# Up-projections of two gated FFNs by seven block products for eight, down-projections woven between them, and buffers that the stages share

## The chip, the cores and the metric

One core of one Trainium2 chip. The metric is the device time of one execution in microseconds; the time before is the median of three runs. Engines: PE is TensorE (PEld its weight loads), DVE is VectorE, ACT is ScalarE, POOL is GpSimd, SP is SyncE, which issues the transfers of weights.

## The reference

A decoder trunk of two layers on 512 tokens of 1024 features, all in float32. Layer 0 mixes by a causal Conformer convolution, layer 1 by sparse attention; each is followed by a gated FFN with 2816 features. All are residual blocks behind an RMS norm. What the change touches:

```python
def conv_ffn(h, w_up, w_dw, b_dw, w_down):
    a, v = jnp.split(h @ w_up, 2, axis=-1)
    return (jax.nn.silu(causal_dwconv(a, w_dw, b_dw)) * v) @ w_down

def reference(x, ...):
    for i in range(DEPTH):
        h = rmsnorm(x, mix_norm_g[i])
        if i % N_MIXERS == 0:
            x = x + conformer_conv(h, ...)
        else:
            x = x + nsa_attention(h, ...)
        x = x + conv_ffn(rmsnorm(x, ffn_norm_g[i]), ...)
    return x
```

`causal_dwconv` in the FFN adds three taps along the tokens, per feature.

## The kernel before

The program runs four stages one after the other: the convolution module (to about 190 us), the first FFN (to about 608), attention (to about 956) and the second FFN. Features lie on the 128 partitions and tokens on the free axis, so the residual stream is eight tiles `x` of 128x512.

Products keep float32 accuracy by an exact split: every weight and activation is the sum of a high part (a cast on ACT, L202 and L208) and a low part (a subtraction on DVE, L203 and L209; in attention some on POOL), and each product is three matmuls: high x high, high x low, low x high (`mm3`, L212 to L215). A load of weights, `load_split`, is a DMA on SP's queue into one of 3 raw buffers, the cast into one of 4 `wh` and the subtraction into one of 4 `wl`. These buffers belong to one pool `wp`, which all stages share.

`ffn` goes through the 22 feature tiles of 128 in chunks of 8, 8 and 6. For a tile f it loads the weights of its two halves (`a` and `v`, L519 on), and multiplies each by the 8 tiles of the normed input: 2 x 8 x 3 = 48 matmuls of 512 columns into PSUM banks pf and pa. The norm's denominators come later: after the first half of tile 0 `finish` and `spread` form 1/rms per token, which multiplies the result (`nrm.b`). Then the activation chain: `a` and `vv` are products of PSUM and `nrm.b` on DVE (L529, L531), the first tap and the bias on ACT (L530), two taps on DVE (L532, L534), Silu on ACT (L536), the product with `vv` on DVE (L537), and the split. When a chunk's tiles are done, each of 8 output tiles m adds up 24 (last chunk 18) matmuls in PSUM bank pb, 8 m's per chunk, and DVE adds it to x[m] (L546). An FFN has 528 such matmuls in all. In the last chunk x[m] goes on to the next stage's norm (`Norm.add`: scaled high part on ACT L231, low part on DVE L232, square on ACT L237, sum of squares on POOL L248), or to the output.

Attention ends with its out-projection: the last 39 matmuls wait for the last head's values (L956 adds their results to x on DVE).

The instructions of all stages go into one program. Within it each engine works through its own list in order, and the lists are set when the program is built: a tile framework takes the operations, and orders ready ones for each engine, so that work of the next loop step or of the next stage can stand before work of this one, as far as buffers of the pools are free. A buffer of a pool is given to the next tile that asks when its last reader is done. The rows of such lists, with the tiles' names and running numbers, are shown below.

Of the kernel before, what the change touches and what calls it, by code (L numbers as in the profile page):

```python
# [18 lines left out]
P = 128  # L19
# [7 lines left out]
CHUNKS = [range(0, 8), range(8, 16), range(16, 22)]  # L27
# [10 lines left out]
# columns of the packed per-feature vectors  # L38
# [14 lines left out]
# columns of the packed token-major tables  # L53
# [11 lines left out]
# order of the work beside the heads: first step and advance per step (a head takes six steps)  # L65
# [59 lines left out]
def _program(tc, A, stop=None, dbg=None):  # L125
    nc = tc.nc
    es = ExitStack()
    with es:
        const = es.enter_context(tc.tile_pool(name="const", bufs=1))
        wp = es.enter_context(tc.tile_pool(name="wp", bufs=1))  # L130
        sp = es.enter_context(tc.tile_pool(name="sp", bufs=51))
        sm = es.enter_context(tc.tile_pool(name="sm", bufs=1))
        psp = es.enter_context(tc.tile_pool(name="psp", bufs=1, space=bass.MemoryType.PSUM))

# [23 lines left out]
        for k in range(KT):  # L158
            nc.sync.dma_start(x[k], A["xT"][k * P:(k + 1) * P, :])
            if k in FIRST_W:  # L160
                raw = wp.tile([P, WPW], F32, tag="raw", name=nm("raw"), bufs=3)
                nc.sync.dma_start(raw[:, :1024], A["pw1"][len(first)])
                first.append(raw)
# [9 lines left out]
        # keeps TensorE's clock up while it has nothing else to do  # L173
        idle = const.tile([P, S], F32R, name="idle")
        nc.vector.memset(idle.bitcast(F32), 0.0)

        def warm(n, tag, after=None):
            """products without a use, that follow the tile `after`"""
# [15 lines left out]
        def load_split(src, n=1024, eng=None):  # L194
            if first:
                raw = first.pop(0)
            else:
                raw = wp.tile([P, WPW], F32, tag="raw", name=nm("raw"), bufs=3)
                nc.sync.dma_start(raw[:, :n], src)
            h = wp.tile([P, WPW], F32R, tag="wh", name=nm("wh"), bufs=4)  # L200
            l = wp.tile([P, WPW], F32R, tag="wl", name=nm("wl"), bufs=4)
# [16 lines left out]
        class Norm:  # L218
# [16 lines left out]
            def square(s, k):  # L235
# [3 lines left out]
                if s.two:  # L239
                    # even tiles on GpSimd, odd ones on VectorE  # L240
# [11 lines left out]
            def sums(s, q, start, stop):  # L252
                """adds q over the features, one column per 128 tokens"""
# [6 lines left out]
            def finish(s):  # L260
                """mean square and its root, per token"""
# [10 lines left out]
        def spread(tok, tag):  # L272
            """the [128, 4] values of the tokens as a row in every partition, in PSUM"""
# [11 lines left out]
        def conv_module(nrm, nxt):  # L285
# [18 lines left out]
            class Unit:  # L304
                """one tile of features: gated unit, then 31 taps shared between the engines: TensorE adds its taps
# [896 lines left out]
```

## Time and profile before

| | us |
|---|---|
| three runs, median (range) | 1336.77 (1333.28 to 1338.4) |
| profiled execution: its time and span | 1333.7 |
| PE busy | 1287.4 (97%) |
| DVE busy | 857.9 (64%) |
| ACT busy | 626.8 (47%) |
| POOL busy | 356.6 (27%) |

The profile gives one execution: for each engine its busy time and number of instructions, the chain of work that ended last followed back to the start, groups of instructions by program line with the mean duration of one, and for any stretch of time the busy time of each engine in it, PE's granted clock (1.00 is full speed) and the share of the DMA engines. In a group or timeline row the brackets, or what stands behind the last bar, tell how long the engine was idle before it and what ended that. A row with x2 joins two instructions.

### The profile page before, as it was taken

The numbers are of one execution on the slowest core, as the hardware profiler recorded it, in microseconds if no ns is written. First come the engines' busy times: TensorE is split into PE (matmuls) and PEld (weight loads), VectorE is DVE, ScalarE is ACT, GpSimd is POOL, SyncE is SP. The second block draws the span as 40 slices with busy tenths as digits, with TensorE's granted clock in tenths as the row PEclk, the third lists the DMA queues.
The fourth block names the chain that finished last, engine by engine and source line by source line (L and its number), as shares of the span: only waits on it lengthen the run. The fifth ranks groups of instructions, "written<-read, shape, count | busy, mean of one in ns | idle before, by whom it ended". The sixth has DMA issues, their size and how long they took to land.

```text
span 1333.7 us, 16982 instructions
## 1 busy us (share of the span) xinstructions
PE 1287.4 (97%) x6314; PEld 1073.6 (80%) x6314; DVE 857.9 (64%) x1429; ACT 626.8 (47%) x1151; POOL 356.6 (27%) x430
## 2 busy tenths in 40 slices
PE   8999789999999999999899999999999999999998
PEld 6887678888888888878789898887788888888886
DVE  6999964665455535554878889788756535553552
ACT  7677543443233323342567788776643313331330
POOL 3669931000000000032467667743400000000000
PEclk9999879999999999999899999999999999999999
DMA  6122101433333333235241111110033322233321
GB/s 235 45 63 64 48 6 58 127 95 95 95 95 95 95 95 96 78 112 149 79 156 35 33 33 50 33 46 33 16 95 95 96 95 94 95 98 95 95 80 76
DMA packets 32321, 109.13 MB, mean 82 GB/s; under 512 B 3696, under 2 KB 4336, under 8 KB 32240
## 3 DMA queue, kind: packets, MB, share of 16 engines
q1 hardware_dynamic: 32240, 108.05, 25.9%
q8 instruction: 50, 0.82, 0.3%
q14 instruction: 31, 0.25, 0.1%
HBM read 103.85 MB, written 2.10 MB: 79 GB/s over the span
## 4 chain that ended last, share of the span: by engine, by line
PE 80%; DVE 9%; POOL 5%; ACT 4%; issue 2%; DMA 0%; SPq 0%; ACTq 0%; POOLq 0%; DVEq 0%
PE pf L213 11%; PE pf L215 11%; PE pf L214 11%; PE pb L213 7%; PE pb L215 7%; PE pb L214 7%; PE pa L215 6%; PE pa L213 6%; PE pa L214 6%; PE po L930 2%; POOL s L344 2%; PE pb L914 1%; DVE s L209 1%; DVE pa L895 1%; DVE s L626 1%
## 5 line engine op out<-in xcount | busy, mean ns | idle before, releaser
L202 ACT CAST wh<-raw 128x1024 fp32r<-128x1024 f32 (+2 forms) x196 | 202.1, 1033 | 398.6 <-PE pb L214 156.2
L203 DVE TENSOR_TENSOR wl<-raw,wh 128x1024 fp32r<-128x1024 f32 (+2 forms) x179 | 223.1, 1248 | 55.2 <-ACT wh L202 54.7
L213 PE MATMUL pf<-s,wh 128*128 128x512 f32 x600 | 236.3, 397 | 6.0 <-DVE s L325 2.3
L215 PE MATMUL pf<-s,wl 128*128 128x512 f32 x600 | 237.9, 396 | 0.5 <-DVE wl L203 0.5
L214 PE MATMUL pf<-s,wh 128*128 128x512 f32 x600 | 238.0, 397 | 0.0
L213 PE MATMUL pa<-s,wh 128*128 128x512 f32 x368 | 145.0, 395 | 0.0
L215 PE MATMUL pa<-s,wl 128*128 128x512 f32 x368 | 145.0, 394 | 0.0
L213 PE MATMUL pb<-s,wh 128*128 128x512 f32 x368 | 144.2, 394 | 0.6 <-DVE x L546 0.6
L215 PE MATMUL pb<-s,wl 128*128 128x512 f32 x368 | 144.7, 393 | 0.0
L214 PE MATMUL pa<-s,wh 128*128 128x512 f32 x368 | 144.6, 393 | 0.0
L214 PE MATMUL pb<-s,wh 128*128 128x512 f32 x368 | 144.5, 393 | 0.0
L213 PEld LDWEIGHTS pf<-s,wh 128*128 128x128 f32 x600 | 113.6, 190 | 31.7 <-DVE s L325 2.6
L248 POOL TENSOR_TENSOR s<-s,s 128x512 f32<-128x512 f32 x18 | 28.2, 1564 | 402.2 <-DVE s L232 333.6
L215 PEld LDWEIGHTS pf<-s,wl 128*128 128x128 f32 x600 | 114.0, 190 | 26.4 <-DVE wl L203 1.0
L214 PEld LDWEIGHTS pf<-s,wh 128*128 128x128 f32 x600 | 114.1, 190 | 25.3 <-issue 0.2
L546 DVE TENSOR_TENSOR x<-pb,x 128x512 f32<-128x512 f32 x48 | 33.0, 692 | 141.0 <-PE pb L215 141.0
L906 POOL TENSOR_SCALAR s<-s,cf,gates 128x128 f32<-128x128 f32 (+3 forms) x128 | 80.1, 633 | 79.1 <-DVE cf L903 68.2
L529 DVE TENSOR_TENSOR s<-pf,s 128x512 f32<-128x512 f32 x44 | 30.4, 691 | 93.3 <-PE pf L215 86.6
L213 PE MATMUL pf<-wh,s 128*128 128x256 f32 (+1 forms) x288 | 83.9, 292 | 4.6 <-DVE v L731 2.9
L214 PE MATMUL pf<-wl,s 128*128 128x256 f32 (+1 forms) x288 | 82.9, 288 | 0.0
L213 PEld LDWEIGHTS pb<-s,wh 128*128 128x128 f32 x368 | 69.2, 188 | 17.0 <-DVE x L546 1.5
L215 PE MATMUL pf<-wh,s 128*128 128x256 f32 (+1 forms) x288 | 82.8, 288 | 0.0
(214 smaller groups left out, 2498.3 us busy)
## 6 DMA issues: line engine op xcount, KB each, us to landing
raw<-in_up_dram SPq DMA_DIRECT2D x88, 512.0 KB, 3.5
raw<-in_dn_dram SPq DMA_DIRECT2D x32, 512.0 KB, 3.5
raw<-in_pw_dram SPq DMA_DIRECT2D x24, 512.0 KB, 3.5
raw<-in_dn_dram SPq DMA_DIRECT2D x16, 384.0 KB, 3.0
raw<-in_win_k_dram SPq DMA_DIRECT2D x8, 536.0 KB, 3.6
raw<-in_win_q_dram SPq DMA_DIRECT2D x8, 512.0 KB, 3.6
raw<-in_cw_dram SPq DMA_DIRECT2D x8, 512.0 KB, 3.7
raw<-in_wout_dram SPq DMA_DIRECT2D x8, 512.0 KB, 3.7
```

Of the source, the lines that this page charges most:

```text
L202: nc.scalar.copy(h[:, :n], raw[:, :n])
L203: (eng or nc.vector).tensor_sub(l[:, :n], raw[:, :n], h[:, :n].bitcast(F32))
L209: nc.vector.tensor_sub(l, src, h.bitcast(F32))
L213: nc.tensor.matmul(out, ah, bh, start=start, stop=False)
L214: nc.tensor.matmul(out, ah, bl, start=False, stop=False)
L215: nc.tensor.matmul(out, al, bh, start=False, stop=stop)
L248: nc.gpsimd.tensor_add(s.acc, s.acc, q)
L344: nc.gpsimd.tensor_add(y[:, k:S], y[:, k:S], z)
L529: nc.vector.tensor_mul(a, pt[0], nrm.b)
L546: nc.vector.tensor_add(x[m], o, x[m])
L906: nc.gpsimd.tensor_scalar(a, a, s.cf[:, c:c + 1], gates[:, i, 3 * s.h + 1 + br:3 * s.h + 2 + br], op0=ALU.mult, op1=ALU.mult)
L930: nc.tensor.matmul(s.o[:, j * P:S], G.v[:, b:b + P], parts[p][:, off:off + n], start=False, stop=p == 1 and (br, j) == (1, 2))
```

## The change

The feature tiles are done in another way, in another order, and the pools are laid out anew.

Seven products for eight. Tiles 0 to 3 are done as before (`classic`). For tiles 4 to 21 (`Pair`) the two halves `a` and `v` of the weights are taken as one 2x2 block matrix: rows are `a` and `v`, columns are the first and last 512 input features; the normed input is a 2x2 block matrix too, its first and last 512 features by the first and last 256 tokens. Strassen's scheme in Winograd's form then needs seven block products in place of eight, each of 4 x 3 matmuls of 256 columns. The sums of input blocks are formed once per FFN by `combine(i)`, i = 0 to 3, while the classic tiles run (on ACT, POOL and DVE, with their splits); since these sums are of the scaled and divided input, the results need no product with `nrm.b`. The sums of weight blocks are formed for each tile on POOL (L633 to L637), split by ACT and DVE, the last (`w4`) with its low part on POOL (L553). The results are added by copies on ACT and adds on DVE out of PSUM, of 256 columns each (L648 to L667), and go through the same activation chain.

Woven downs. Chunks are 4, 5, 5, 4 and 4 tiles. The first chunk's 8 down-projections (12 matmuls each) stand ahead of the pairs; the later ones are spread over the pairs of the next chunk, one or two behind each, and the last chunk's stand at the end. A pair's third and fourth steps (`third`, `fourth`) follow the first and second steps of the next.

Pools. Each stage opens pools of its own and closes them at its end, so the same bytes serve another stage after it: the FFNs have 4 raw, 6 `h` and 6 `l` buffers and 2 of each for the sums, attention's tables and buffers lie in a pool `at`.

Numbers of instructions: PE 6024 to 7318 in its list, DVE 1428 to 1605, ACT 1006 to 1302.

```diff
-CHUNKS = [range(0, 8), range(8, 16), range(16, 22)]
+CHUNKS = [range(0, 4), range(4, 9), range(9, 14), range(14, 18), range(18, 22)]
+COMBINE = [[], [0], [], [1, 2, 3]]
+AHEAD = 8
+NORM_AT = [(0, 5), (1, 3)]
...
-        wp = es.enter_context(tc.tile_pool(name="wp", bufs=1))
+        def open_stage(name, *pools):
+            stage["es"] = ExitStack()
+            for n in pools:
+                stage[n] = stage["es"].enter_context(tc.tile_pool(name=f"{name}_{n}", bufs=1, reuse_waits="tile"))
...
+            def combine(i):
+                if i % 2 == 0:
+                    combine.b11 = slot(F32R), slot(F32R)
+                y = [slot(), slot()]
+                for j in range(2):
+                    k = i + j * KT // 2
+                    nc.scalar.activation(y[j], x[k], AF.Copy, scale=v(nrm.g, k))
+                    nc.gpsimd.tensor_mul(y[j], y[j], nrm.b)
+                (y11, y12), (y21, y22) = ((t[:, 0:HS], t[:, HS:S]) for t in y)
+                t = buf("S", 3 * HD2, F32, 2)
+                t12, t34 = t[:, 0:S], t[:, S:2 * S]
+                nc.gpsimd.tensor_sub(t12[:, 0:HS], y12, y11)
+                nc.vector.tensor_sub(t34[:, 0:HS], y22, y12)
+                nc.gpsimd.tensor_sub(t12[:, HS:S], y22, t12[:, 0:HS])
+                nc.gpsimd.tensor_sub(t34[:, HS:S], y21, t12[:, HS:S])
+                h, l = (t[:, i % 2 * HS:i % 2 * HS + HS] for t in combine.b11)
+                nc.scalar.copy(h, y11)
+                nc.vector.tensor_sub(l, y11, h.bitcast(F32))
+                B[0].append((h, l))
+                for t, (p, q) in ((y[1], (1, 2)), (t12, (4, 5)), (t34, (6, 3))):
+                    h, l = split(t)
...
+            def products(o, w, n, start=False):
+                for i in range(KT // 2):
+                    wh, wl = (t[:, i * P:(i + 1) * P] for t in w)
+                    bh, bl = B[n][i]
+                    for j, (p, q) in enumerate(((wh, bh), (wh, bl), (wl, bh))):
+                        nc.tensor.matmul(o, p, q, start=start and i + j == 0, stop=i == KT // 2 - 1 and j == 2,
+                                         skip_group_check=True)
+            class Pair:
+                def __init__(s, f):
...
+                    s.w1 = parts(raw1)
+                    nc.gpsimd.tensor_add(s1, a21, a22)
+                    nc.gpsimd.tensor_sub(s2, s1, a11)
+                    nc.gpsimd.tensor_sub(a21, a11, a21)
+                    s.w2 = parts(sums[:, 0:D])
+                    nc.gpsimd.tensor_sub(s4, a12, s2)
+                    s.w3 = parts(raw2)
+                    s.w4 = parts(s4, "4", HD2, 2, nc.gpsimd)
...
+                def first(s):
+                    s.al, be = ps("pa")[:, 0:HS], ps("po")[:, 0:HS]
+                    s.u, s.a, s.vv = slot(), slot(), slot()
+                    products(s.al, s.half(s.w1, 0), 0, True)
+                    nc.scalar.copy(s.u[:, 0:HS], s.al)
+                    products(be, s.half(s.w1, 1), 1, True)
+                    nc.vector.tensor_add(s.a[:, 0:HS], be, s.u[:, 0:HS])
+                def second(s):
+                    s.ga = ps("pf")[:, 0:HS]
+                    products(s.al, s.half(s.w2, 1), 5)
+                    nc.scalar.copy(s.u[:, HS:S], s.al)
+                    products(s.ga, s.half(s.w2, 0), 4, True)
+                    nc.scalar.copy(s.vv[:, HS:S], s.ga)
+                def third(s):
+                    products(s.al, s.half(s.w3, 0), 6)
+                    nc.vector.tensor_add(s.vv[:, HS:S], s.al, s.vv[:, HS:S])
+                def fourth(s):
+                    products(s.ga, s.w4, 2)
+                    nc.vector.tensor_add(s.a[:, HS:S], s.ga, s.u[:, HS:S])
+                    products(s.al, s.half(s.w3, 1), 3)
+                    nc.scalar.copy(s.vv[:, 0:HS], s.al)
+                    activate(s.f, s.a, s.vv)
...
+            for f in CHUNKS[0]:
+                classic(f)
+                for i in COMBINE[f]:
+                    combine(i)
+            todo = [(0, m) for m in range(KT)]
+            for _ in range(AHEAD):
+                down(*todo.pop(0))
+            last = None
+            for ch, fs in list(enumerate(CHUNKS))[1:]:
+                for n, f in enumerate(fs):
+                    p = Pair(f)
+                    p.first()
+                    if last:
+                        last.third()
+                    p.second()
+                    if last:
+                        last.fourth()
+                    last = p
+                    if n == 0 and ch > 1:
+                        todo += [(ch - 1, m) for m in range(KT)]
+                    for _ in range(-(-len(todo) // (len(fs) - n))):
+                        down(*todo.pop(0))
...
+            if stg[:3] == "ffn":
+                open_stage(stg, "raw", "h", "l", "S")
+            elif stg == "attn":
+                open_stage(stg, "wh", "at", "wl", "raw")
```

How the lists stand now, at three places. In them `h_` and `l_` are parts of weights in the FFNs, `S_` a buffer of sums (of weight blocks, or of input blocks in `combine`), `s_` a 128x512 slot, `pf_`, `pa_`, `po_` and `pb_` PSUM banks, `x_81` to `x_88` the eight tiles of x.

First, POOL's list in the first FFN of the changed kernel, from `combine(3)` to the end of pair 0's sums (tile 4):

```order
L596 TENSOR_TENSOR s_2420<-s_2420,s_2080 128x512
L596 TENSOR_TENSOR s_2421<-s_2421,s_2080 128x512
L600 TENSOR_TENSOR S_2426<-s_2420 128x256
L633 TENSOR_TENSOR S_2609<-raw_2607 128x512
L602 TENSOR_TENSOR S_2426<-s_2421,S_2426 128x256
L634 TENSOR_TENSOR S_2609<-S_2609,raw_2605 128x512
L635 TENSOR_TENSOR raw_2607<-raw_2605,raw_2607 128x512
L603 TENSOR_TENSOR S_2426<-s_2421,S_2426 128x256
L637 TENSOR_TENSOR S_2609<-raw_2605,S_2609 128x512
L553 TENSOR_TENSOR l_2627<-S_2609,h_2626 128x512
```

Before, POOL's list has nothing between the first FFN's norm and the next one's; now the sums of the first pair are woven with those of the last `combine`.

Second, ACT's list a little later in the same place of the changed kernel, where the first pair's parts are cast:

```order
L228 CAST s_2437<-S_2426 128x512
L552 CAST h_2617<-S_2609 128x1024
L552 CAST h_2622<-raw_2607 128x1024
L552 CAST h_2693<-raw_2688 128x1024
L228 CAST s_2441<-S_2426 128x512
L552 CAST h_2626<-S_2609 128x512
L648 COPY s_2632<-pa_2630 128x256
L657 COPY s_2634<-pf_2661 128x256
L655 COPY s_2632<-pa_2630 128x256
```

The second weight block's cast (`h_2617`) stands behind the casts of `combine`, and the fourth's (`h_2626`) behind three more and ahead of the copies that free the PSUM banks.

Third, DVE's list where the second FFN starts. Before (out-projection adds at L956, `wl_8976` the low part of the second FFN's first weights, the rest attention's last heads):

```order
L956 TENSOR_TENSOR x_74<-pf_8586,x_74 128x512
L203 TENSOR_TENSOR wl_8976<-raw_8973,wh_8975 128x1024
L903 RECIPROCAL cf_8305<-sums_8304 128x1
L209 TENSOR_TENSOR s_8429<-pb_8423,s_8428 128x512
L956 TENSOR_TENSOR x_75<-pf_8655,x_75 128x512
L903 RECIPROCAL cf_8305<-sums_8304 128x1
L956 TENSOR_TENSOR x_76<-pf_8718,x_76 128x512
L895 ISA pa_8455,mn_8447<-pa_8455,tab 128x128
```

And in the changed kernel (L1119 adds, L252 the norm's low parts):

```order
L1119 TENSOR_TENSOR x_87<-pf_10223,x_87 128x512
L252 SCALAR_TENSOR_TENSOR s_10202<-x_85,vec,s_10201 128x512
L1119 TENSOR_TENSOR x_88<-pf_10238,x_88 128x512
L252 SCALAR_TENSOR_TENSOR s_10217<-x_86,vec,s_10216 128x512
L252 SCALAR_TENSOR_TENSOR s_10232<-x_87,vec,s_10231 128x512
L252 SCALAR_TENSOR_TENSOR s_10247<-x_88,vec,s_10246 128x512
L553 TENSOR_TENSOR l_10271<-raw_10268,h_10270 128x1024
L553 TENSOR_TENSOR l_10315<-raw_10312,h_10314 128x1024
```

The first weights' low part stood among earlier out-projection work; now it stands behind the last x add and the last norm part.

## Rows read from the trace of the kernel before

**Rows 1.** The page: busy time of the engines, and the chain that ended last by engine.

```profile
PE 1287.4 (97%) x6314; PEld 1073.6 (80%) x6314; DVE 857.9 (64%) x1429; ACT 626.8 (47%) x1151; POOL 356.6 (27%) x430
PE 80%; DVE 9%; POOL 5%; ACT 4%; issue 2%; DMA 0%; SPq 0%; ACTq 0%; POOLq 0%; DVEq 0%
```

**Rows 2.** Windows: the two FFNs; columns as the first line names them.

```profile
core 0: us, PE busy (x) PEld busy (x) DVE busy (x) ACT busy (x) POOL busy (x), PEclk, DMA share, GB/s
250.00:576.00 326.00, 326.00 (x1418) 265.82 (x1417) 169.38 (x207) 104.29 (x125) 0.00 (x0) 1.00 0.30 93
956.00:1334.00 378.00, 373.77 (x1630) 304.26 (x1628) 193.77 (x235) 120.07 (x147) 11.12 (x7) 1.00 0.29 91
```

**Rows 3.** Windows, PE alone: 256-column products in attention, 512-column ones in FFN 0.

```profile
627.10:638.40 11.30, 11.30 (x96) 1.00 0.63 181
262.00:570.00 308.00, 308.00 (x1337) 1.00 0.31 93
```

**Rows 4.** Groups by line: out<-in (partitions x elements) xcount | busy us, mean ns | idle before.

```profile
L202 ACT CAST wh<-raw 128x1024 fp32r<-128x1024 f32 x172 | 180.2, 1049 | 353.7 <-PE pf L214 141.7 <-PE pb L214 138.3 <-PE pa L214 54.4
L208 ACT CAST s<-s 128x512 fp32r<-128x512 f32 x76 | 46.8, 620 | 65.4 <-DVE s L537 35.4 <-DVE s L332 17.2 <-DVE s L626 9.4
L722 ACT ACTIVATE t<-pf,nt 128x256 f32<-128x256 f32 x16 | 7.6, 474 | 10.2 <-PE pf L215 10.1
L530 ACT ACTIVATE s<-s,vec 128x512 f32<-128x512 f32 x44 | 35.9, 816 | 7.4 <-DVE s L529 6.8
L536 ACT ACTIVATE s<-s 128x512 f32<-128x512 f32 x44 | 27.8, 632 | 81.9 <-DVE s L534 81.9
L532 DVE SCALAR_TENSOR_TENSOR s<-s,vec,s 128x511 f32<-128x511 f32 x44 | 32.9, 747 | 0.6 <-ACT s L530 0.6
L537 DVE TENSOR_TENSOR s<-s,s 128x512 f32<-128x512 f32 x44 | 30.4, 691 | 6.3 <-ACT s L536 2.8
```

**Rows 5.** Timeline of POOL, 55 to 139 us: start, us, engine, line, operation.

```profile
55.02 2.64 POOL L344 TENSOR_TENSOR s<-s,s 128x506 f32<-128x506 f32 x2
...
131.07 2.66 POOL L344 TENSOR_TENSOR s<-s,s 128x509 f32<-128x509 f32 x2
133.70 1.30 POOL L398 TENSOR_TENSOR s<-s,s 128x512 f32<-128x512 f32 x1
134.96 4.05 POOL L344 TENSOR_TENSOR s<-s,s 128x507 f32<-128x507 f32 x2
```

**Rows 6.** Timeline of DVE, 56 to 138 us.

```profile
56.91 1.83 DVE L203 TENSOR_TENSOR wl<-raw,wh 128x1024 fp32r<-128x1024 f32 x1
...
134.94 1.22 DVE L203 TENSOR_TENSOR wl<-raw,wh 128x1024 fp32r<-128x1024 f32 x1
136.07 0.72 DVE L321 SCALAR_TENSOR_TENSOR pa<-s,vec,pa 128x487 f32<-128x487 f32 x1
136.70 1.15 DVE L332 SCALAR_TENSOR_TENSOR s<-s,vec,s 128x512 f32<-128x512 f32 x1
```

**Rows 7.** Timeline of ACT, DVE and POOL where the second FFN starts.

```profile
956.64 1.04 ACT L202 CAST wh<-raw 128x1024 fp32r<-128x1024 f32 x1
...
961.60 1.18 DVE L232 SCALAR_TENSOR_TENSOR s<-x,vec,s 128x512 fp32r<-128x512 f32 x1
...
963.30 2.89 DVE L232 SCALAR_TENSOR_TENSOR s<-x,vec,s 128x512 fp32r<-128x512 f32 x2
...
966.71 1.71 DVE L203 TENSOR_TENSOR wl<-raw,wh 128x1024 fp32r<-128x1024 f32 x1
...
958.35 8.99 POOL L248 TENSOR_TENSOR s<-s,s 128x512 f32<-128x512 f32 x5 [0.67 <-ACT s L237]
```

**Rows 8.** Windows, PE alone, around the last head; the fifth number is the granted clock.

```profile
948.00:951.00 3.00, 0.90 (x6) 1.00 0.00 0
951.00:955.00 4.00, 4.00 (x11) 0.59 0.00 0
```

**Rows 9.** The page, DMA issues: count, KB each, us to landing.

```profile
raw<-in_up_dram SPq DMA_DIRECT2D x88, 512.0 KB, 3.5
```

More of the change, by code (lines that the diff above doesn't have):

```diff
@@ L148, in small @@
             return sm.tile([P, w], dt, tag=tag, name=nm(tag), bufs=bufs)
+        open_stage("conv", "raw", "gap", "wh", "wl")
+        gap = stage["gap"].tile([P, GAP], F32, name="gap")
         vec = const.tile([P, NVEC], F32, name="vec")
@@ new lines, in ffn, with buf, load, parts @@
+            up, dn = A[f"up{li}"], A[f"dn{li}"]
+            def buf(tag, w, dt, bufs):
+                return stage[tag if tag in stage else "S"].tile([P, w], dt, tag=tag, name=nm(tag), bufs=bufs)
+            def load(src, n=D):
+                raw = buf("raw", WPW, F32, 4)[:, 0:n]
+                nc.sync.dma_start(raw, src)
+                return raw
+            def parts(raw, tag="", w=D, bufs=6, eng=None):
+                n = raw.shape[1]
+                h, l = (buf(t + tag, w, F32R, bufs)[:, 0:n] for t in "hl")
+                nc.scalar.copy(h, raw)
+                (eng or nc.vector).tensor_sub(l, raw, h.bitcast(F32))
+                return h, l
@@ new lines, in classic @@
+            def classic(f):
+                pt = []
+                for half, tag in ((0, "pf"), (1, "pa")):
+                    wh, wl = parts(load(up[2 * f + half]))
+                    o = ps(tag)
+                    pt.append(o)
+                    for k in range(KT):
+                        sl = slice(k * P, (k + 1) * P)
+                        mm3(o, wh[:, sl], wl[:, sl], nrm.h[k], nrm.l[k], k == 0, k == KT - 1)
+                        if f == 0 and (half, k) in NORM_AT:
+                            (nrm.finish, nrm.spread)[NORM_AT.index((half, k))]()
+                a, vv = slot(), slot()
+                nc.vector.tensor_mul(a, pt[0], nrm.b)
+                nc.vector.tensor_mul(vv, pt[1], nrm.b)
+                activate(f, a, vv)
@@ new lines, in down @@
+            def down(ch, m):
+                fs = CHUNKS[ch]
+                wh, wl = parts(load(dn[ch * KT + m, :, :len(fs) * P], len(fs) * P))
+                o = ps("pb")
+                for j, f in enumerate(fs):
+                    sl = slice(j * P, (j + 1) * P)
+                    mm3(o, wh[:, sl], wl[:, sl], gs[f][0], gs[f][1], j == 0, j == len(fs) - 1)
+                nc.vector.tensor_add(x[m], o, x[m])
+                if ch == len(CHUNKS) - 1:
+                    if nxt is not None:
+                        nxt.add(m)
+                    else:
+                        nc.sync.dma_start(A["out"][m * P:(m + 1) * P, :], x[m])
@@ L554, in attention, with small @@
+            last.third()
+            last.fourth()
+            for m in range(KT):
+                down(len(CHUNKS) - 1, m)
         def attention(nrm, nxt):
+            def small(w, tag, bufs=2, dt=F32):
+                return stage["at"].tile([P, w], dt, tag=tag, name=nm(tag), bufs=bufs)
             def weights(nme, i, n=1024):
                 return load_split(A[nme][i], n, nc.gpsimd if LP[UNITS.index((nme, i))] else nc.vector)
-            tab = const.tile([P, NTAB], F32, name="tab")
+            tab = stage["at"].tile([P, NTAB], F32, name="tab")
@@ L861, in cmp_probs @@
                 G.pc = split(tp)
-            vbuf = [const.tile([P, 2 * NB * P], F32R, name=f"v{n}") for n in range(NVB)]
             mask = tb("mask")
```

129 lines of the change are left out of this document (53 added, 76 removed).

## The prediction

> **What bounds the kernel now.** I read the page's first part and its chain first [rows 1]. TensorE is busy 1287.4 us of the 1333.7 us span, and 80% of the chain that ended last is PE. Then the windows by stage [rows 2]: in the first FFN's body (250 to 576) PE is busy 326.00 of 326.00 us and GpSimd does nothing; in the second (956 to 1334) it is 373.77 of 378.00, with DVE at 193.77, about half. The reader is to see that both FFNs, some 800 us, are bound by the number of PE columns alone, with half of DVE, two thirds of ACT and all of GpSimd free. The change spends these to buy columns. The execution read here took 1333.7 us, its span; that is 3.1 below the median of 1336.8, so I sum against 1333.7 and add 3.1.
>
> **What PE gains.** A 512-column product costs 308.00/1337 = 0.2304 us in the first FFN, and 96 products of 256 columns in attention, each with a weight load of its own, cost 11.30/96 = 0.1177 us [rows 3]; the median distance from start to start in these two stretches is 0.2306 and 0.1186, which I take. A feature tile before: 2 halves x 8 x 3 = 48 products of 512 columns, 11.07 us. As a Pair: 7 block products x 4 x 3 = 84 of 256 columns, 9.96 us. 1.11 us for each of 18 tiles in 2 FFNs: **-40.2 us**. The down products keep their number (528 in an FFN), and conv and attention keep their order.
> The Trainium skill ("TensorE: Matmul & The Clock Gate", section "Back-to-back issue gap") gives the isolated gap as N/2.4 + 2.5 ns, 216 and 109 ns, from which I estimate 42.7 us; the rows are longer at both widths, and I keep theirs.
>
> **What the other engines take on, for a Pair.** GpSimd gets five 512-column operations (L633 to L637 and the low part of the fourth weight block, L553). Its row for 512 columns and two SBUF inputs is 1.30 us [rows 5]: 6.5 us. DVE: three low parts of 1024 columns at 1.22, two taps at 0.75, the product with `vv` and the split's low part at 0.69 [rows 4], together 6.55 us; three adds from PSUM of 256 columns, an estimated 0.4 us each by L537's 0.69 for 512, and its share of the downs. ACT: three casts at 1.05, one of 512 at 0.62, three copies at some 0.47, and the activation's 0.82 + 0.63 + 0.62, about 7.3 [rows 4]. Each alone is under PE's 9.96. Not so the two together. In [rows 5] and [rows 6] GpSimd's L344 starts at 134.96, 0.02 us after DVE's L203, and two of them take 4.05 us where two took 2.66 just before; DVE's L332 beside them takes 1.15 instead of 0.75. So each runs while the other stands, though DVE operations with one PSUM input (L321, 0.72) are untouched. At the start of the second FFN L232 takes 1.18 to 1.45 beside GpSimd's L248, and L203 1.71 [rows 7].
> The Trainium skill says the same and more strictly ("SBUF — State Buffer", section "Who interferes with whom"): a VectorE instruction with two SBUF inputs and a GpSimd instruction share one port pair under an exclusive lock, held for a whole instruction. By that rule everything above adds up, which is the second rival; the rows agree that they exclude each other, but the one that waited then needs less than its full time: the second L344 ends at 139.01, 1.16 after L332 (for 1.30), and a L203 that began under an L344 ended 1.08 after it (58.74 and 57.66; for 1.22), and by the same rows a 512-column one on DVE some 0.55 (for 0.69 to 0.75).
>
> **What it costs, place by place.**
> - Ramp, from the last of the four unpaired tiles to pair 0, in each FFN. PE has 96 down products (22.1 us) and 24 of 256 columns (2.8), 25 us, to cover `combine` 1 to 3 and pair 0's block sums. GpSimd: 3 x (2 x 1.30 + 3 x 0.65 for 256 columns, an estimate by half the row) + 5 x 1.30 = 20.2. DVE's operations with two SBUF inputs there: 8.3 in the combines, four low parts of weights 4.9, the last tile's activation 2.9, 16.1 us. All serial 36.3, 11 late; with the shorter times 17.9 + 13.5, 6 late; with no exclusion the chain from GpSimd over DVE to ACT, where the cast that the second weight block needs stands behind the combines' casts and ahead of three others (the second place shown above), and the last tile's split copies are 3.5 to 5 late. Bounds 0 to 11; I take 6, the shorter serial time, because the rows show that shorter time: **+12** for both.
> - Chunk 1: five pairs with no downs between, 9.96 us of PE each, against 6.5 + 6.55 = 13.05 serial, or 5 x 1.16 + 3 x 1.08 + 4 x 0.55 = 11.2 with the shorter times. Loss over five pairs 0, 6 or 15 us; raw and sum buffers let GpSimd run up to two pairs ahead, which gives part of it back. I take 2.5, between none and the shorter serial time: **+5** for both. In chunks 2 to 4 a pair has one or two downs of 15 products (3.46 us) beside it, so PE has 13.4 to 16.9 us, against 11.2 and 0.8 to 1.6 for the downs' low parts, or 14.7 at full times: covered, 0; without that cover 1 to 2 us a pair.
> - Tail: the last pair's outputs leave an activation chain of about 6.2 us for 5.6 us of cover: **+1.8** for both, bounds 0 to 4.
> - Start of the second FFN. Before, its first weights were cast at 956.64 and its products were woven among the out-projection [rows 7]; PE had no gap after 951. Now the first up weights' raw buffer lies on bytes of the second last out-projection's weights, so the transfer (3.5 us, [rows 9]) starts late, and on DVE `l_10271` stands behind every x add and the last three norm parts (the third place shown above). PE's last out-projection product ends near 962; x_88's add 0.69, three parts at 1.2 beside GpSimd's squares, the low part 1.5: 967.8. Idle 5.5, and then the clock. After a PE that was busy 0.90 of 3.00 us the granted clock was 0.59 over 951 to 955 [rows 8], the lower level of 1.2 GHz for 3.4 us, which costs 1.7. **+7**, bounds 3 to 10.
> - First FFN to attention: the first attention weights' low part now stands behind x_88's add, some 2 us of PE: **+2**, bounds 0 to 4.
> - One more half-clock stretch of 1.7 after the ramps' idle: **+1.7**, bounds 0 to 7.
> - Transfers: 88 up loads of 512 KB as before [rows 9], and the downs in 40 loads instead of 24, the bytes the same. DMA was busy 0.29 and 0.30: 0, and nothing below, since SP does nothing else.
> The sum: -40.2 + 12 + 5 + 1.8 + 7 + 2 + 1.7 = -10.7; 1323.0, and with the 3.1 **1326 us**. By the bounds of its terms this case reaches from 1314 to 1338.
>
> **Rivals.**
> - *PE stays the bound* (0.18). Exclusion costs only waiting engines, since the queues run ahead by two pairs; only the second FFN's start (3) is left: -37, **1300 us**. For it: chunks 2 to 4 cover even the serial times on most pairs, and GpSimd's order runs up to two pairs ahead. Against it: chunk 1 has no downs and the ramp has one chain.
> - *DVE and GpSimd exclude each other for whole instructions* (0.21), slower: their sum, not PE, is the bound wherever a pair has under 13.05 us of PE. Ramps 22, chunk 1's 15 twice is 30, the other terms 12.5: 64.5 - 40.2 = +24, **1361 us**. It decides once chunk 1's pairs take over 12 us. A milder form, with the shorter times in chunk 1 and nothing ahead (0.11): 12 + 12 + 12.5 - 40.2 = -4, **1333 us**, no change. For it: [rows 5] to [rows 7]. Against: both engines wait on PE for long in each pair, when they need not collide.
> - *256-column products run at the weight load's pace* (0.03): every product has its own load, and 84 loads stand for 48. At over 0.132 us a product a tile gains nothing. [rows 3] speaks against it with 0.1177, each with its load. Time: with the losses of 29.5 and no gain, 1366 us.
>
> **How the numbers follow.** The forecast has 0.47; the four others 0.18, 0.21, 0.11 and 0.03. A measurement of this kernel tells about 0.5%, 6.7 us, from no change: faster is under 1330.1, slower over 1343.5. Faster: 0.18 + three quarters of 0.47 + a little of 0.11 = 0.55. Same: the other quarter, and 0.08 of the milder form's, 0.2. Slower: 0.21 + 0.03 + 0.01 = 0.25. The range from 1298 to 1360 leaves out some 0.08 of the clean case and 0.12 of the serial one and the last.
>
> **What would show it.** In the profile after: 0.118 to 0.120 us a 256-column product, or the first sum falls. PE gaps of 4 to 8 us before pair 0's fourth block product (`first`/`second`, L655 to L657), released by ACT or DVE from GpSimd's L633 to L637; if these gaps are none the clean rival holds. In chunk 1 PE busy under 95% with DVE and GpSimd rows lengthened (L553 on GpSimd over 2 us) speaks for the serial rival, PE at 99% against it. In the second FFN a gap of about 5 us near 960 whose releaser is DVE L553, followed by a clock near 0.5. The forecast is wrong if chunks 2 to 4 show PE gaps of over 0.5 us a pair, or if attention's or conv's time moves by over 3 us.

## The result, and the profile after

The changed kernel takes **1368.5 us** (median of four runs, 1367.4 to 1368.6) against 1335.9 before: 1.0245 times as long, 95% interval 1.0227 to 1.0262. The forecast was 1326, faster. The profiled execution has a span of 1366.8 us, 33.1 above [rows 1]'s kernel. The page's first part and its chain, which answer to [rows 1]:

```profile
PE 1278.2 (94%) x7610; PEld 1129.7 (83%) x7610; DVE 1039.7 (76%) x1605; ACT 755.5 (55%) x1447; POOL 695.6 (51%) x650
PE 67%; DVE 14%; POOL 8%; ACT 5%; issue 5%; DMA 0%; SPq 0%; POOLq 0%; ACTq 0%; DVEq 0%
```

The span and mean granted clock of the core, of the changed kernel, then of the kernel before:

```profile
core 0: 1366.8 us, clock 0.966
```

```profile
core 0: 1333.7 us, clock 0.983
```

These lines already divide the 33.1. PE's idle time is 1366.8 - 1278.2 = 88.6 us, before 1333.7 - 1287.4 = 46.3: **+42.3**. What the lower clock takes, as (1 - clock) x span, is 46.5 and before 22.7: **+23.8**. What is left, 33.1 - 42.3 - 23.8, is **-33.0**: the columns saved, with whatever else changed in TensorE's pace. So the saving came, and two things ate it twice over. In the chain DVE and POOL went from 14% together to 22%.

Where they lie is seen in windows of the changed kernel, which answer to [rows 2] (columns as there; the third number from the end is the granted clock):

```profile
283.00:301.70 18.70, 14.30 (x66) 10.41 (x64) 15.27 (x20) 10.80 (x19) 11.32 (x10) 1.00 0.25 84
301.70:358.00 56.30, 48.12 (x313) 44.42 (x314) 48.91 (x39) 27.25 (x44) 55.03 (x32) 0.90 0.25 81
358.00:586.00 228.00, 227.72 (x1572) 213.33 (x1571) 171.16 (x203) 115.72 (x188) 101.20 (x64) 0.99 0.32 103
609.00:640.00 31.00, 26.21 (x108) 21.07 (x108) 10.49 (x11) 5.44 (x7) 9.58 (x11) 0.89 0.49 153
640.00:720.00 80.00, 67.07 (x497) 64.68 (x496) 58.52 (x104) 45.44 (x89) 38.55 (x40) 0.91 0.35 114
966.50:982.50 16.00, 12.38 (x42) 9.42 (x41) 11.14 (x16) 9.69 (x16) 7.44 (x5) 0.79 0.14 43
982.50:1036.00 53.50, 51.24 (x222) 42.80 (x223) 35.81 (x44) 24.94 (x34) 8.44 (x8) 0.94 0.34 115
1036.00:1064.00 28.00, 24.87 (x114) 19.29 (x112) 24.12 (x30) 14.09 (x23) 20.78 (x17) 1.00 0.17 57
1064.00:1113.00 49.00, 37.87 (x267) 36.55 (x267) 43.08 (x31) 23.78 (x38) 46.07 (x27) 0.88 0.28 93
1113.00:1343.00 230.00, 229.73 (x1576) 214.98 (x1575) 169.75 (x203) 116.01 (x188) 98.66 (x63) 0.99 0.30 95
```

Chunks 2 to 4 (the third and the last row) are full: 227.72 of 228.00. The ramps (first and eighth row) idle 4.4 and 3.1 us. **Chunk 1** (second and ninth row) idles 8.2 and 11.1, and its clock of 0.90 and 0.88 takes another 5.6 and 5.9. Its last half-clock stretches run 2.4 and 5.2 us into the rows behind (the last two rows of the PE windows below) and cost 1.2 and 2.6 more there. In chunk 1 POOL is busy 55.03 of 56.30 us and DVE 48.91: two engines with slack by their own times are full. How, the timelines of the same stretch show, POOL first, then DVE (they answer to [rows 5] and [rows 6]; columns as there):

```profile
345.14 2.15 POOL L634 TENSOR_TENSOR S<-S,raw 128x512 f32<-128x512 f32 x1
347.25 1.74 POOL L635 TENSOR_TENSOR raw<-raw,raw 128x512 f32<-128x512 f32 x1
348.95 2.27 POOL L637 TENSOR_TENSOR S<-raw,S 128x512 f32<-128x512 f32 x1
351.18 1.74 POOL L553 TENSOR_TENSOR l<-S,h 128x512 fp32r<-128x512 f32 x1
...
346.07 1.77 DVE L562 SCALAR_TENSOR_TENSOR s<-s,vec,s 128x511 f32<-128x511 f32 x1
347.76 2.32 DVE L553 TENSOR_TENSOR l<-raw,h 128x1024 fp32r<-128x1024 f32 x1
350.00 1.77 DVE L564 SCALAR_TENSOR_TENSOR s<-s,vec,s 128x510 f32<-128x510 f32 x1
351.69 2.32 DVE L553 TENSOR_TENSOR l<-S,h 128x1024 fp32r<-128x1024 f32 x1
353.93 1.77 DVE L567 TENSOR_TENSOR s<-s,s 128x512 f32<-128x512 f32 x1
```

Read the ends: POOL ends at 347.29, 348.99, 351.22, 352.92, and DVE at 347.84, 350.08, 351.77, 354.01. They take turns without a gap; each row holds its own time and the wait for the other's. DVE's low part takes 2.32 for 1.22, its taps 1.77 for 0.75, POOL's 512 columns 1.74 to 2.27 for 1.30. PE waits for both, and the timeline of PE shows its longer gaps with their releasers in brackets, three of the four over 1 us in chunk 1 of the first FFN, then those at the starts of attention and of the second FFN:

```profile
338.67 0.50 PE L619 MATMUL pa<-s,h 128*128 128x256 f32 x2 [3.74 <-DVE s L661]
354.06 0.39 PE L619 MATMUL pf<-s,l 128*128 128x256 f32 x1 [1.04 <-DVE l L553]
356.68 0.50 PE L619 MATMUL pa<-s,h 128*128 128x256 f32 x2 [1.17 <-ACT s L648]
...
611.96 0.50 PE L235 MATMUL pf<-s,wl 128*128 128x512 f32 x1 [2.33 <-DVE wl L223]
632.94 0.50 PE L233 MATMUL pf<-s,wh 128*128 128x512 f32 x1 [2.46 <-DVE s L768]
984.76 1.57 PE L277 MATMUL po<-ones,s 128*128 128x1 f32 x8 [3.78 <-POOL s L268]
```

The first gap's releaser is an add of 256 columns from PSUM (0.41 us). It stood behind four lengthened operations on DVE; the third gap's is a copy on ACT, which stood behind a cast (L228) that had waited 2.31 us for DVE's product L567, 1.77 us long for 0.69. What the idle time does to the clock, in windows of PE alone (first the stretch of 84 products of one pair, which answers to [rows 3], then the gap of 3.74 us and what follows, then the second FFN's start, last the half-clock stretches behind chunk 1 of each FFN; they answer to [rows 8]):

```profile
448.05:458.00 9.95, 9.95 (x84) 1.00 0.37 124
334.90:338.70 3.80, 0.06 (x2) 1.00 0.66 243
340.00:347.00 7.00, 5.94 (x30) 0.51 0.25 75
980.90:984.80 3.90, 0.12 (x2) 1.00 0.75 266
984.80:992.00 7.20, 7.20 (x26) 0.53 0.71 221
358.00:360.40 2.40, 2.40 (x14) 0.50 0.45 137
1113.00:1118.20 5.20, 5.20 (x26) 0.50 0.20 63
```

After a gap of 3.8 us with hardly a product PE runs some 7 us at 0.51 to 0.53, its lower level of 1.2 GHz: a gap costs nearly its length again.

Attention's start lost most of the rest. Before, PE was busy 35.20 of 35.20 us from the last x add on and now 26.21 of 31.00 at a clock of 0.89; in the 80 us behind it idle and clock take 12.9 + 7.2 us, before 9.6 + 4.8. From the FFN's last x add to attention's own last one the stage takes 373.9 us, before 362.0. The kernel before there, in windows:

```profile
604.80:640.00 35.20, 35.20 (x216) 31.40 (x215) 19.48 (x31) 11.41 (x18) 8.70 (x8) 1.00 0.49 136
640.00:720.00 80.00, 70.37 (x524) 67.08 (x523) 62.52 (x127) 51.56 (x114) 53.59 (x68) 0.94 0.34 107
```

### The profile page after: what moved, and what is told of

Read it like the earlier page. It is cut to its first block, busy times and chain, and to the rows that moved or that the text cites. A ratio compares the mean times of both kernels' runs of the same rounds, so it can differ in the third digit from the quotient of the medians.

```text
span 1366.8 us, 20524 instructions
## 1 busy us (share of the span) xinstructions
PE 1278.2 (94%) x7610; PEld 1129.7 (83%) x7610; DVE 1039.7 (76%) x1605; ACT 755.5 (55%) x1447; POOL 695.6 (51%) x650
## 4 chain that ended last, share of the span: by engine, by line
PE 67%; DVE 14%; POOL 8%; ACT 5%; issue 5%; DMA 0%; SPq 0%; POOLq 0%; ACTq 0%; DVEq 0%
PE pa L619 13%; PE pf L619 6%; PE pf L233 6%; PE pf L235 6%; PE pf L234 6%; PE pb L233 6%; PE pb L234 5%; PE pb L235 5%; PE po L619 3%; DVE l L553 2%; DVE s L229 2%; PE po L1093 2%; POOL s L364 2%; PE pb L1077 1%; DVE wl L223 1%
## 5 line engine op out<-in xcount | busy, mean ns | idle before, releaser
L553 DVE TENSOR_TENSOR l<-raw,h 128x1024 fp32r<-128x1024 f32 (+2 forms) x168 | 211.6, 1267 | 52.9 <-ACT h L552 50.8
L619 PE MATMUL pa<-s,h 128*128 128x256 f32 x1152 | 220.9, 290 | 13.9 <-DVE s L661 7.3
L619 PEld LDWEIGHTS pa<-s,h 128*128 128x128 f32 x1152 | 186.8, 197 | 18.5 <-DVE s L661 7.7
L552 ACT CAST h<-raw 128x1024 fp32r<-128x1024 f32 (+2 forms) x168 | 143.0, 863 | 106.0 <-PE pa L619 22.9
L619 PE MATMUL pa<-s,l 128*128 128x256 f32 x576 | 166.7, 290 | 1.8 <-DVE l L553 1.8
L233 PE MATMUL pb<-s,h 128*128 128x512 f32 x352 | 137.6, 396 | 8.5 <-ACT s L228 4.8
L234 PE MATMUL pb<-s,h 128*128 128x512 f32 x352 | 138.6, 394 | 0.0
L235 PE MATMUL pb<-s,l 128*128 128x512 f32 x352 | 137.7, 391 | 0.0
L633 POOL TENSOR_TENSOR S<-raw 128x512 f32<-128x512 f32 x36 | 53.4, 1484 | 132.2 <-DMA raw<-in_up_dram 114.4
L619 PEld LDWEIGHTS pa<-s,l 128*128 128x128 f32 x576 | 113.9, 198 | 2.8 <-DVE l L553 2.7
L233 PE MATMUL pf<-s,wh 128*128 128x512 f32 x248 | 100.5, 414 | 8.1 <-DVE s L768 2.5
L235 PE MATMUL pf<-s,wl 128*128 128x512 f32 x248 | 101.3, 409 | 2.9 <-DVE wl L223 2.9
L229 DVE TENSOR_TENSOR s<-s,s 128x512 fp32r<-128x512 f32 x84 | 80.7, 964 | 28.8 <-ACT s L228 28.5
L228 ACT CAST s<-s 128x512 fp32r<-128x512 f32 x84 | 51.8, 620 | 89.8 <-DVE s L567 54.0
L234 PE MATMUL pf<-s,wh 128*128 128x512 f32 x248 | 101.3, 408 | 0.0
L553 POOL TENSOR_TENSOR l<-S,h 128x512 fp32r<-128x512 f32 x36 | 58.3, 1620 | 70.5 <-ACT h L552 70.5
```

What stands on the lines that cost most here:

```text
L228: nc.scalar.copy(h, src)
L229: nc.vector.tensor_sub(l, src, h.bitcast(F32))
L233: nc.tensor.matmul(out, ah, bh, start=start, stop=False)
L234: nc.tensor.matmul(out, ah, bl, start=False, stop=False)
L235: nc.tensor.matmul(out, al, bh, start=False, stop=stop)
L552: nc.scalar.copy(h, raw)
```

## The experiments

Theory 1: VectorE and GpSimd exclude each other, so moving work to GpSimd took it from VectorE. Its rival, theory 2: the chain from sums over casts to products is too long, whoever does the sums. Theory 3: pools that share bytes delay the first weights of attention and of the second FFN.

**The sums on VectorE (sums_dve).** All five GpSimd operations of a Pair:

```diff
-                    nc.gpsimd.tensor_add(s1, a21, a22)
-                    nc.gpsimd.tensor_sub(s2, s1, a11)
-                    nc.gpsimd.tensor_sub(a21, a11, a21)
+                    nc.vector.tensor_add(s1, a21, a22)
+                    nc.vector.tensor_sub(s2, s1, a11)
+                    nc.vector.tensor_sub(a21, a11, a21)
...
-                    s.w4 = parts(s4, "4", HD2, 2, nc.gpsimd)
+                    s.w4 = parts(s4, "4", HD2, 2)
```

> A Pair's five GpSimd operations (four block sums, low part of w4) move to VectorE, nothing else changes. Theory 1 (exclusion): the changed kernel loses about 34 us in chunk 1 of the two FFNs (gaps of 7.9 and 10.9 us and half clock over 13.7 and 17 us, so 15 more), because VectorE and GpSimd run by turns; by start-to-start distances VectorE alone needs 3 x 1.14 + 5 x 0.60 + 2 x 0.67 + 2 x 0.61 + 3 x 0.33 = 10.0 us a pair, as long as TensorE's 10.08, so most of the loss goes: about 1338 us. Theory 2 (the length of the chain from the sums over the casts to the products, and the order on ScalarE): VectorE, already at 76%, gets 3 us a pair more in one chain, and the time rises to 1375 us or more.

Measured: 1345.7 us, 1.007 of before (1.0044 to 1.0096). VectorE got 180 more operations and the kernel is 22.8 us shorter: theory 2 falls, theory 1 stands, 8 us short of its number. Of the 23 us between the two profiled executions 19 lie in the two FFNs and 4 in attention, which the edit doesn't touch: in the eight kernels that start attention late it takes from 366 to 376 us, so a total can move by some us without anything that was edited. Groups by line of 350 to 600 us in this kernel:

```profile
L553 DVE TENSOR_TENSOR l<-raw,h 128x1024 fp32r<-128x1024 f32 x27 | 33.0, 1221 | 7.0 <-ACT h L552 6.7
L562 DVE SCALAR_TENSOR_TENSOR s<-s,vec,s 128x511 f32<-128x511 f32 x16 | 11.9, 746 | 2.4 <-ACT s L561 2.2
L633 DVE TENSOR_TENSOR S<-raw 128x512 f32<-128x512 f32 x12 | 8.3, 691 | 5.7 <-DMA raw<-in_up_dram 5.6
```

Every operation is back at its own time (1221, 746), and a sum costs 0.69 on VectorE, where on GpSimd it took 1.30 and kept VectorE waiting for some 1.14 of them (the ends above). A likely reason for the 8 us: in chunk 1 VectorE is now nearly full by itself, busy 50.79 of 51.50 us, while PE idles 5.6:

```profile
300.50:352.00 51.50, 45.93 (x315) 43.17 (x316) 50.79 (x72) 28.57 (x46) 6.24 (x5) 0.93 0.28 89
```

**The sums left out (no_sums).**

```diff
-                    nc.gpsimd.tensor_add(s1, a21, a22)
-                    nc.gpsimd.tensor_sub(s2, s1, a11)
-                    nc.gpsimd.tensor_sub(a21, a11, a21)
-                    s.w2 = parts(sums[:, 0:D])
-                    nc.gpsimd.tensor_sub(s4, a12, s2)
+                    s.w2 = parts(raw2)
...
-                    s.w4 = parts(s4, "4", HD2, 2, nc.gpsimd)
+                    s.w4 = parts(a12, "4", HD2, 2, nc.gpsimd)
```

> The four block sums of a Pair are left out: the second and the fourth weight blocks are taken from the raw weights, so GpSimd keeps one of five operations and the casts wait for no sum. Theory 1 and 2 both: chunk 1's loss goes, about 1334 us, and what is left is TensorE's gain of 36 less the ramps, tails and stage starts. If chunk 1 still shows gaps of over 2 us and half clock, the cause is neither, but the order on TensorE or the PSUM copies.

Measured: 1340.0 us (1.0037, 1.0024 to 1.0051). Chunk 1 is full:

```profile
303.50:355.00 51.50, 50.77 (x385) 48.71 (x386) 41.61 (x52) 32.07 (x54) 11.75 (x9) 1.00 0.27 85
```

So neither PE's order nor the PSUM copies cost anything there that shows. The 6 us over the expectation are in attention, which is 6 us longer here than in the experiment above, from one last x add to the next; why its order comes out so was not followed.

**The old products with the new pools and chunks (classic).**

```diff
-COMBINE = [[], [0], [], [1, 2, 3]]
+COMBINE = [[], [], [], []]
...
-                    p = Pair(f)
-                    p.first()
...
+                    classic(f)
```

> All 22 feature tiles by the old eight products, no combine and no Pair; chunks, woven downs and the pools by stage stay as in the changed kernel. Theory 3 (pools that share bytes delay the start of attention by about 14 us and that of the second FFN by about 7): 1336 + 21 = 1357 us, with no gap inside the FFNs. Rival: the late starts come from the Pairs' tail (last sums and fourth blocks hold buffers), then 1336 to 1340 us.

Measured: 1345.0 us (1.0074, 1.0051 to 1.0097), between the two numbers. The late starts are all there, with no Pair in the kernel (windows, all engines: attention's start, the second FFN's start):

```profile
598.40:632.00 33.60, 28.80 (x118) 23.34 (x119) 11.57 (x15) 6.79 (x8) 10.03 (x11) 0.85 0.50 151
959.00:980.00 21.00, 16.83 (x61) 13.77 (x61) 18.79 (x21) 14.57 (x21) 10.37 (x7) 0.75 0.58 195
```

4.8 and 4.2 us idle, and 5.0 and 5.3 by the clock. That it is still only 9 us over before is a gain that nobody had counted: its 512-column products are closer together (next but two).

**Everything on VectorE (all_dve).** As the first, and in `combine`:

```diff
-                    nc.gpsimd.tensor_mul(y[j], y[j], nrm.b)
+                    nc.vector.tensor_mul(y[j], y[j], nrm.b)
...
-                nc.gpsimd.tensor_sub(t12[:, 0:HS], y12, y11)
+                nc.vector.tensor_sub(t12[:, 0:HS], y12, y11)
```

(and the two subtractions behind it).

> As sums_dve, and the GpSimd operations of combine (two products with the denominators and three subtractions each) move to VectorE as well, so that GpSimd does nothing in the FFNs but the norm's squares. Theory 1: the ramps gain 2 to 5 us against sums_dve, about 1334 us. Theory 2: VectorE's longer list makes the ramps later, 5 us or more above sums_dve.

Measured: 1340.5 us (1.0041, 1.0026 to 1.0057), 5.2 less than with the sums alone, as theory 1 has it and not theory 2. That the ramps gained it is not shown: the two intervals overlap, and of the 5.4 us between the profiled executions only 2.4 lie in the FFNs.

**Other buffer distances (classic_1072).** On the kernel with the old products:

```diff
-            def parts(raw, tag="", w=D, bufs=6, eng=None):
+            def parts(raw, tag="", w=WPW, bufs=6, eng=None):
```

> classic with h and l buffers of 1072 columns for 1024, so that one begins 4288 bytes behind the other as in the kernel before, and not 4096. In classic every 512-column product of the FFNs starts 226 to 227 ns behind the one before, in the kernel before 226 to 241, mean 230.6, by weight buffer. If the buffers' addresses set this, the mean rises to about 230.6 and the time by 2 x 1584 x 3.9 ns = 12.4 us to 1357. Rival: more buffers or another order of work set it, then 1345 us as classic.

Measured: 1360.6 us (1.0186, 1.0165 to 1.0207), 15.6 more. The same 270 us of the first FFN, PE alone, first with 4096 bytes from buffer to buffer, then with 4288, then in the kernel before (4288):

```profile
300.00:570.00 270.00, 270.00 (x1193) 1.00 0.29 91
```

```profile
300.00:570.00 270.00, 270.00 (x1166) 1.00 0.30 90
```

```profile
300.00:570.00 270.00, 270.00 (x1173) 1.00 0.30 93
```

270/1193 = 226.3 ns a product, 231.6 and 230.2. The expectation (230.6) holds; the addresses set it. So the late starts, with whatever the new chunks cost beside them, come to what theory 3 said, 9 + 2 x 1584 x 3.9 ns = 21 us. Which addresses are good ones was not tried.

**Downs woven into chunk 1 (weave_dve)**, and **first weights ahead of the stage (pre_dve)**, each on all_dve, then **both (pre_weave_dve)**:

```diff
-COMBINE = [[], [0], [], [1, 2, 3]]
-AHEAD = 8
+COMBINE = [[0], [1], [2], [3]]
+AHEAD = 3
```

```diff
-                    wh, wl = parts(load(up[2 * f + half]))
+                    wh, wl = pre.pop(2 * f + half, None) or parts(load(up[2 * f + half]))
...
             for m in range(KT):
                 down(len(CHUNKS) - 1, m)
+            if li == 0:
+                for i in range(2):
+                    pre["wkv", i] = parts(load(A["wkv"][i]))
...
             for nme in sorted(work):
                 drain(work[nme])
+            for i in range(2):
+                pre[i] = load_split(A["up1"][i])
```

> all_dve with AHEAD 3 for 8 and one combine behind each unpaired tile: five of the first chunk's downs are woven between chunk 1's five pairs. In all_dve chunk 1 still idles TensorE 4.6 us in the first FFN and 4.8 in the second, with half clock that costs 3.4 and 1.7 more. If TensorE lacks cover there (10.1 us of products a pair beside 10.0 us of VectorE), a down of 2.8 us a pair ends that: 1326 us. Rival: the ramp loses the cover of five downs and takes the gain back: 1340 us or more.

> all_dve, and the first two weight units of attention are loaded and split in buffers of the first FFN's pools, those of the second FFN's first tile in attention's, before the pools close; nothing else changes. Theory 3 (late first weights, because the pools share bytes, leave TensorE without work while the norm's sum is formed): the gaps at the two starts and their half clock go, 15 to 20 us of the 21.7 that classic shows: about 1323 us. Rival: the norm's chain to the denominators sets the starts, since three PSUM banks fill up before it is through: 1335 us.

> Both edits on all_dve. They touch different stretches, so their gains should add: about 1309 us by theories 1 and 3, 26 us under the kernel before. If one of the two gives nothing by itself, this one shows the other's alone.

Measured: woven 1335.7 (1.0016, 0.9997 to 1.0035), 4.8 less and not 14; ahead 1331.3 (0.9966, 0.995 to 0.9982), 9.1 less and not 15 to 20; both **1326.1** (0.993, 0.9905 to 0.9954), 14.4 less: they add (4.8 + 9.1 = 13.9), and the kernel is 0.7% faster than before. The 4.8 alone is hardly clear of the noise (the intervals overlap); that it comes again on top of the weights ahead, as 5.2, speaks for it. With the first weights ahead alone, attention's start is full, 31.65 of 32.00 at a clock of 1.00:

```profile
600.00:632.00 32.00, 31.65 (x195) 27.93 (x194) 19.61 (x32) 9.89 (x16) 11.00 (x15) 1.00 0.61 162
```

Attention then takes 360.3 us from x add to x add, for 369.1 in all_dve. At the second FFN the wait only moved, which is why the gain stays under 15: PE no longer stands at the norm's sums, but 3.24 us for the cast of the second tile's weights. Their transfer began at 968.5 us, after SP had waited for a product of PE.

```profile
974.23 0.50 PE L234 MATMUL pf<-s,h 128*128 128x512 f32 x1 [3.24 <-ACT h L553]
```

In the kernel with both, chunk 1 is full too (second row), but the ramp (first row) idles 8.4 us at a clock of 0.73, as the rival of the woven downs said:

```profile
283.00:302.00 19.00, 10.58 (x39) 7.79 (x37) 17.10 (x32) 10.30 (x17) 0.00 (x0) 0.73 0.00 0
302.00:345.00 43.00, 43.00 (x316) 40.81 (x315) 41.53 (x63) 24.86 (x42) 0.00 (x0) 1.00 0.45 135
```

Its timeline there:

```profile
292.68 1.22 PE L234 MATMUL pb<-s,h 128*128 128x512 f32 x2 [6.39 <-ACT s L229]
```

That row is the ramp's long gap: a down waits for tile 3's split (L229), whose activation stood on VectorE behind the combine of tile 2.

**A GpSimd that nobody waits for (sums_dve_dummy).** On sums_dve:

```diff
                     s.w1 = parts(raw1)
+                    d = slot()
+                    nc.gpsimd.tensor_add(d, a11, a12)
+                    for _ in range(4):
+                        nc.gpsimd.tensor_add(d, d, nrm.b)
```

> sums_dve, and GpSimd gets five 512-column additions for each Pair whose result nobody reads: they start when the first raw weights are there, and nothing waits for them. Theory 1 (exclusion): VectorE stands for most of each of them, some 5 x 1.2 us a pair, so chunk 1 and the ramps lose at least what the changed kernel lost there, and chunks 2 to 4 too wherever TensorE has little cover: 1375 us or more. If engines only count by their own load, GpSimd was idle there, and the time stays at sums_dve's 1346.

Measured: 1463.8 us, 118.1 more, for 180 additions without a reader: 0.66 us of the whole kernel for each. No count of loads explains that; exclusion does, and it is the cleanest showing of it. The additions also hold a slot and a raw buffer, but in neither FFN does an operation of PE, ACT or DVE wait for one of them; of the loads one does in each, 4.4 and 4.5 us. In 350 to 600 us of this kernel:

```profile
L636 POOL TENSOR_TENSOR s<-s,s 128x512 f32<-128x512 f32 x52 | 86.1, 1656 | 4.1
L637 DVE TENSOR_TENSOR S<-raw 128x512 f32<-128x512 f32 x14 | 15.4, 1102 | 10.3 <-DMA raw<-in_up_dram 10.2
```

A sum on VectorE takes 1102 ns for 691; the adds to x, with one input from PSUM, keep their time (681).

**The combines earlier**, on pre_dve: COMBINE [[0], [1], [], [2, 3]] with AHEAD 6, and conv's buffers at 4096 bytes (early_combine), then with AHEAD 5 and conv as it was (ahead5):

```diff
-COMBINE = [[], [0], [], [1, 2, 3]]
-AHEAD = 8
+COMBINE = [[0], [1], [], [2, 3]]
+AHEAD = 5
```

> pre_dve with combine(0) and (1) behind the first two unpaired tiles, (2) and (3) behind the last, AHEAD 6 (two downs woven into chunk 1), and conv's weight buffers 4096 bytes apart as in the FFNs. pre_weave_dve's ramp idles 6.4 us and lies at half clock for 10.2, because the combine behind tile 2 stands ahead of tile 3's activation on VectorE; here nothing stands there, and 72 of 96 down products cover the last two combines. Theory 1: ramp and chunk 1 together lose under 5 us an FFN: 1320 us. Conv: 576 products at up to 4 ns less, 2 us: 1318 us. Rival: the ramp's cover is too short again, 1326 us.

> pre_dve with AHEAD 5 and the combines behind tiles 0, 1 and (two) 3, conv as in the changed kernel: three downs woven into chunk 1, 60 down products ahead for the last two combines. early_combine (AHEAD 6) idles 5.2 us in the first ramp and 3.3 to 3.6 in chunk 1. If cover in chunk 1 is what counts, 1324 us or less; if the ramp loses what chunk 1 gains, 1328 us.

Measured: 1328.3 (0.9954, 0.9941 to 0.9967) and 1324.7 (0.9916, 0.9882 to 0.9949; its runs lie between 1321 and 1332). Neither can be told from the 1326.1 of the kernel with both edits; conv's buffers gave nothing that shows in the total, though the distance of conv's products did follow them: between 190 and 233 us its median is 227 ns in early_combine and 231 in pre_dve.

**Cover without moving the sums (pre_weave)**: the two edits (AHEAD 3, first weights ahead) on the changed kernel itself.

> pre_weave_dve's two edits on the changed kernel itself, with its sums, low parts and combines on GpSimd as they were. Theory 1: the engines still take turns, but a pair of chunk 1 now has 12.9 us of TensorE for some 12.4 of turns, so chunk 1's 34 us go for the most part and the starts' 9 to 14 too: about 1335 us, and what is above pre_weave_dve's 1326 is the ramp, where GpSimd and VectorE take turns with less cover. If cover doesn't matter and only the place of the sums does: 1355 us.

Measured: 1356.5 us (1.016, 1.0132 to 1.0188): the rival's number. Chunk 1 still loses 5.5 idle and 3.5 by the clock in these windows, although each of its pairs has a down beside it, and the ramp gets worse (windows: ramp, chunk 1):

```profile
283.00:308.00 25.00, 11.88 (x43) 8.35 (x44) 17.80 (x22) 11.80 (x19) 15.90 (x14) 0.79 0.00 0
308.00:358.00 50.00, 44.48 (x306) 41.73 (x305) 41.63 (x39) 24.56 (x41) 37.27 (x22) 0.93 0.37 116
```

13.1 us idle in the ramp for 4.4 in the changed kernel; the same edits idle 8.4 there with everything on VectorE, so part of it is the cover that the ramp gave up. This cover for PE didn't repair two engines that take turns: 30.4 us lie between this kernel and the same one with GpSimd's work on VectorE.

## Why the prediction was wrong, step by step

- **TensorE's gain, -40.2**: held nearly. 84 products in 9.95 us, 83 distances of 0.1199 for the 0.1186 taken: 36 x (11.07 - 10.07) = -36.0, and -33.0 is left in the page's sums. (36 x 1.11 is 40.0, not 40.2.)
- **Ramp, +12 for both FFNs**: 4.4 + 3.1 = 7.5 idle at a clock of 1.00, within the bounds of the step.
- **Chunk 1, +5 for both, and one half-clock stretch, +1.7**: this failed. Measured 8.2 + 11.1 = 19.3 idle and 5.6 + 1.2 + 5.9 + 2.6 = 15.3 by the clock: 34.6 for 6.7. The prediction named the exclusion, had its shorter times right (1.14 for POOL's 512 columns, 1.09 for the low part, 0.55 for a tap, by the ends listed above) and came to 11.2 us a pair against 10; it then took more than half of that back because GpSimd "runs up to two pairs ahead". It didn't: the ramp was late itself, and POOL and DVE, busy 98% and 87% of chunk 1, had no time left in which to get ahead. GpSimd's operations for a pair then take 2.0 us each and their chain of five 10 us, so small adds and copies on DVE and ACT that free a PSUM bank or a slot stand behind lengthened operations (the gap of 3.74 behind L661). The half clock was priced for one stretch; six lie in and just behind the two chunks 1.
- **Chunks 2 to 4, 0; tail, +1.8**: held: 0.3 us idle in each FFN, and 1.18 us at each tail.
- **Start of the second FFN, +7**: the size nearly held (the gap of 3.8, and 3.4 + 3.2 by the clock, less 1.7 before: 8.7; another gap of 2.09 before the last out-projection was there before too), the waiting place did not: PE stood at the norm's sums (L277, released by POOL L268), not at DVE's L553. No product was there to fill that wait; with the first tile's weights ahead it is gone.
- **First FFN to attention, +2**: this failed too. 4.8 idle and 3.4 by the clock in the first 31 us, and 5.7 more in the 80 behind it: 13.9. The prediction had named this as a sign of being wrong, attention's time moving by over 3 us: it is 373.9 for 362.0. I priced the one low part behind x_88's add. What counted was that no attention product was left to stand beside the norm's chain, so that what follows came later: attention's first 256-column product starts 31.6 us behind the last x add, before 22.4. The run with the first weights ahead fills this stretch (31.65 of 32.00), and attention takes 360.3 us there.
- The sum of the misses: 27.9 in chunk 1 and the clock, 11.9 in attention, 4.2 in the gain and -4.5 in the ramps are 39.5 of the 42 us between 1326 and 1368, and the second FFN's start and the tails add 2. That it closes so well is partly chance: by the page's sums 3 us less were gained, and smaller terms the other way were not followed.
- **The range.** Added up as listed, the bounds of the terms reach from 1300 to 1374 us, and not from 1314 to 1338. The 1368.5 lies inside the first; attention and the clock left their own bounds all the same.
- **The rivals.** The one that 256-column products run at the weight load's pace, 1366 us, came nearest by its number and has the wrong cause: they are 0.1199 us apart, and it needed over 0.132. The one of whole-instruction exclusion, 1361 us, is near by other numbers too, and so by luck in part: it had 22 for the ramps (7.5), 30 for chunk 1 (19.3 idle, and 15.3 by a clock that it priced at 1.7) and 2 for attention (13.9). That the engines exclude each other for whole instructions is right. By the Trainium skill ("SBUF — State Buffer", section "SBUF: two separate sides") the shared port pair is an exclusive lock, and whichever of a VectorE operation with two SBUF inputs and a GpSimd operation that reads SBUF starts first has it for the whole instruction. The rows at 345 to 354 us agree: the ends alternate, each at least 0.55 (taps), 1.09 (low parts) or 1.14 us (POOL) behind the other engine's. Those are the shorter times of [rows 5] and [rows 6], 0.1 to 0.2 us a turn under the full ones; they held, and what failed is the stock that was to make up for them.

## What to carry to other kernels

An idle GpSimd is no free engine beside a VectorE whose operations have two inputs from SBUF: price a GpSimd operation at nearly its own time on VectorE as well, and compare with VectorE doing it (here 0.69 against 1.14 of VectorE's time). Before a stretch without cover, ask what stock the slack engines bring into it; "they can run ahead" holds only if they were early, and a gap of some 4 us is paid nearly twice through the clock. Where stages share bytes, load and split the next stage's first weights in the old stage's buffers, so that products stand beside the norm's chain between them; here one tile's weights were too few at the second FFN.

## What the runs showed of the hardware that I had not expected

The start addresses of weight buffers set the distance of 512-column products: 226.3 ns with buffers 4096 bytes apart, 231.6 with 4288, all else the same, and 15.6 us of the kernel. And 180 GpSimd additions whose result nobody reads cost 118.1 us.
